# Stores of attention results move from SyncE's DMA queue to GpSimd's, and their readers wait for the landing

## The chip, the cores and the metric

The kernel runs on one core of a Trainium2 chip. Five engines work side by side, each through its own list of instructions, strictly in order: TensorE (PE; its weight loads are listed apart as PEld), VectorE (DVE), ScalarE (ACT), GpSimd (POOL) and SyncE (SP), which computes nothing and issues DMA transfers. The metric is the device time of one execution in microseconds (us). Three runs of the kernel before gave 1774.26, 1767.66 and 1772.58 us, a median of 1772.58.

## What is computed

One decoder layer over 2048 tokens of width 1024: RMSNorm, one projection to 3724 columns, four groups of four attention heads with different rules (A, B, C, D), a SiLU gate, an output projection, and the residual sum.

```python
h = rms_norm(x, norm_w[layer]) @ w_in[layer]
o_a = dilated_attention(...)   # A: windows 128, 512, 2048 with strides 1, 4, 16, merged by their softmax sums
o_b, _ = banded_attention(...) # B: sliding window of 128, shared keys, learned sinks
o_c = diff_attention(...)      # C: two causal softmax maps, p0 - lam * p1, then a norm per head
o_d = nsa_attention(...)       # D: compressed + selected top-16 blocks + window of 512, sigmoid gates
y = concatenate([merge(o_a), merge(o_b), merge(o_c), merge(o_d)]) * silu(silu_gate)
x = x + y @ w_out[layer]
```

## The kernel before

Activations and weights are split into a high and a low part (`xh`, `xl`, `wb`), so that each product is three matmuls. GpSimd makes `xh` and `xl` from the loaded input tile `xt` (lines 571 and 577), two pairs for each tile of 128 tokens. The projection of a group runs over 16 such tiles; its queries, keys, values and gates go to DRAM and are read back by the attention.

The attention runs as units of one to four query tiles: scores on TensorE, bias and row maximum on VectorE (line 952), exp on ScalarE (1050), transposes of the probabilities on TensorE (393), their split into `ph` and `pl` on ScalarE and VectorE (399 and 403), and products with the values (422). In group C VectorE also combines the two maps (line 1066, with two inputs in SBUF). At a unit's end the result is turned (435), and GpSimd scales it (448; in C also 1099 to 1102, in D also 1553, in A 1887 and 1890). Then it is stored to one of four DRAM tensors: `yC`, `yD`, `yA`, `yB`, 32, 32, 8 and 16 stores. The last part, the output projection, loads them back as `xt<-yC`, `xt<-yD` and so on, multiplies them with the gate on GpSimd (2113), turns them and multiplies with `w_out` (2159). Its first half (C and D) writes a partial sum `acc_d`, its second half (A and B) adds to it and writes the output.

The order of everything is set while the program is built. A planner in the kernel keeps a clock for each engine in a dictionary `T`, adds an assumed duration for each instruction that it emits, and always picks the next step whose inputs are ready by these clocks. `defer(ready, f)` queues work for an assumed time. The projection of the next group, and at the end the output projection, are "fillers": they are emitted where attention has nothing ready. So a changed clock anywhere changes the order on all engines; the hardware then follows that order, waiting by semaphores where an assumption was wrong. The stretches of the trace: projection of C to about 120 us, attention C beside the projections of C, D and A to about 720, D's window and compressed branches beside A's and B's to about 1040, D's selected branch beside B's to 1350, A's wide windows beside the output projection to about 1510, A's window of 128 and B to 1720, and the rest of the output projection to the end.

Every DMA is issued by `mv` on SyncE's queue (line 156). SyncE waits there until what the transfer reads has been written and the place that it writes is free, and what stands behind waits with it. To lessen this the planner emits a result's store late: in C and D 4500 ns (`LATE`) after it should be ready by the clocks, in A and B 1500 ns (`LATE2`), or when the next unit closes. `dstored`, `astored` and `stored` count the stores issued; the output projection's loads of `y` are emitted once the counts are complete. They then stand behind the stores in the same queue, and wait there for their landing.

Of the kernel before, what the change touches and what calls it, by code (L numbers as in the profile page):

```python
# [102 lines left out]
def tile_hybrid_heads(ctx, tc, a):  # L103
# [50 lines left out]
    def mv(dst, src, after=0.0):  # L154

        sy.dma_start(dst, src)
        T["SP"] = max(T["SP"], T["PE"], after) + 475.0
        run = 4.0 * min(dst.shape[-1], src.shape[-1])
        T["DMA"] = max(T["DMA"], T["SP"] + 650.0) + 4.0 * math.prod(dst.shape) / run * (4.7 + 0.0456 * run) / 16
        return T["DMA"] + 1900.0  # L160

    filling = [False]
# [326 lines left out]
    def dv(t):  # L489
        return t.rearrange("(t p) c -> p t c", p=128)  # L490
# [493 lines left out]
    def group_c():  # L984
      with tc.tile_pool(name="cs", bufs=1) as cs, tc.tile_pool(name="cw", bufs=2) as cw:
# [34 lines left out]
        def make(h, t0):  # L1020
# [66 lines left out]
            def close(ot):  # L1087
                O = cw.tile([128, 2, 64], F32, name="O")
                rd = cw.tile([128, 4], F32, name="rd")
                V.reciprocal(rd[:, 0:2], den[:, :, 0])  # L1090
                e = o_turn(ot, 2, O, rd[:, 0:2])
                sq = KK[1][:, 0:64]
                ss = rd[:, 2:4]

                def rest():
                    for i in range(2):
                        A.activation(sq, O[:, i], AF.Square, accum_out=ss[:, i:i + 1])
                    e2 = op("ACT", 2 * av(64, 1), e)
                    G.tensor_scalar(ss, ss, 1.0 / 64, EPS, op0=OP.mult, op1=OP.add)
                    G.tensor_tensor(ss, ss, expo[:, :2], op=OP.pow)  # L1100
                    G.tensor_tensor(O, O, ss.unsqueeze(2).broadcast_to([128, 2, 64]), op=OP.mult)
                    G.tensor_tensor(O, O, subln.unsqueeze(1).broadcast_to([128, 2, 64]), op=OP.mult)
                    e3 = op("POOL", 1966.0, e2)
                    last.append(defer(e3 + (LATE if (h, t0) != (3, 14) else 0.0), lambda: mv(dv(y_d["C"])[:, t0:t0 + 2, h * 64:h * 64 + 64], O)))
                while last:
                    last.pop(0).run()
                last.append(defer(e, rest))
# [131 lines left out]
    def group_d():  # L1239
      with tc.tile_pool(name="dk", bufs=1) as dk:  # L1240
# [132 lines left out]
        with tc.tile_pool(name="ds", bufs=1) as ds_:  # L1373
# [133 lines left out]
          with tc.tile_pool(name="dx", bufs=2) as dx:  # L1507
            start("A", before_a(), more)
            PR = Rows([dx.tile([128, S], F32, name="prow%d" % i, bufs=1) for i in range(4)])
            def make(h, t0):  # L1510
# [33 lines left out]
                def close(ot):  # L1544
# [8 lines left out]
                    G.tensor_tensor(O, O, yp, op=OP.add)  # L1553
                    e = op("POOL", 420.0, e)

                    def store():
                        mv(dv(y_d["D"])[:, ts, h * 64:h * 64 + 64], O)
                        dstored[t0] = dstored.get(t0, 0) + 1
                    closing(defer(e + (LATE if (h, t0) != (3, 14) else 0.0), store))

                u = unit(dx, s1, causal_banks(rows, t0, lambda b: VS[:, b, :]), 2,
                         lambda bi: max(rt[0], rt[1]) if len(rt) == 2 else None, close)
# [53 lines left out]
    def group_ab():  # L1616
      with tc.tile_pool(name="aw", bufs=2) as aw, tc.tile_pool(name="as", bufs=1) as as_:
# [241 lines left out]
            u["v"] = lambda vb: As[m][2][:, q0 + vb - As[m][7], :]  # L1859
            return u  # L1860

        pend, pend2 = [], []

        def join(m, q0, h, e):
            R, Y = As[m][3], As[m][8]
# [15 lines left out]
            def two(e1):  # L1881
# [9 lines left out]
                e3 = op("POOL", 2027.0, e2)  # L1891

                def go():
                    e = mv(dv(y_d["A"])[:, q0:q0 + 4, h * 64 - 64:h * 64 + 64], Y)
                    release(As[m - 1][5], e)
                    release(As[m][5], e)
                    astored[q0] = astored.get(q0, 0) + 2
                    defer(T["PE"] + 500.0, a_more)
                if h % 2:
                    pend2.append(defer(e3 + LATE2, go))  # L1900
            while pend2:
                pend2.pop(0).run()
            defer(e, one)


# [23 lines left out]
        def make_b(n):  # L1929
# [48 lines left out]
            def close(ot):  # L1978
# [10 lines left out]
                op("DVE", 300.0, e)  # L1989
                e = o_turn(ot, 4, O, den)  # L1990

                def store():
                    mv(dv(y_d["B"])[:, t0:t0 + 2, g * 128:g * 128 + 128], O.rearrange("p (t j) d -> p t (j d)", j=2))
                    stored[t0] = stored.get(t0, 0) + 1
                while blast:
                    blast.pop(0).run()
                blast.append(defer(e + LATE2, store))

            need = lambda: max(at("s"), bready.get((g, t0), INF))
            u = unit(as_, [(need, lambda: scores(0)), (need, lambda: scores(1))], banks, 4,  # L2000
# [64 lines left out]
    def out_proj():  # L2065
# [76 lines left out]
        for n, (t, halves, _, dst) in enumerate(JOBS):  # L2142
            at_["part"] = p0
            prepare()
            for c in range(2):
# [22 lines left out]

                def go(xr=xr, hk=hk, t=t, c=c, dst=dst):
                    release(hk, mv(dst[t * 128:(t + 1) * 128, c * 512:(c + 1) * 512], xr))  # L2170
                defer(e, go)
            p0 += len(halves)

    with tc.tile_pool(name="first", bufs=1) as fp:
# [63 lines left out]
```

## Time and profile before

| | us |
|---|---|
| median of three runs | 1772.58 |
| the profiled execution | 1773.27 |
| its span, first to last instruction | 1771.5 |
| PE busy | 1709.5 (97%) |
| DVE busy | 1338.3 (76%) |
| ACT busy | 1072.3 (61%) |
| POOL busy | 692.8 (39%) |
| DMA, share of 16 engines | 55.8% |

An engine is busy when at least one of its instructions runs. The matmuls overlap (one begins while the last drains), so a busy TensorE is not one at its peak. A wait is the idle time of an engine just before an instruction, put down to what came last of the things the instruction waited for. SyncE's waits are listed apart, since its queue has no busy time. The chain of waits follows the work that ended last back to the start.

### The profile page before, as it was taken

The page shows a single profiled execution, that of the slowest core. Times are in us where ns is not written, and L with a number is a line of the kernel's source. Part 1 is how long each engine was busy: PE and PEld are TensorE (multiplying, and loading weights), DVE is VectorE, ACT ScalarE, POOL GpSimd, SP SyncE. Part 2 cuts the span into 40 slices and gives each one's busy share as a digit, 9 for nine tenths or more (in the row PEclk, how much of TensorE's full clock was granted, in tenths as well). Part 3 has the DMA queues.
Part 4 walks back from the last instruction along what each step waited for, and adds up shares of the span by engine and source line. Part 5 has one row for each costly group of instructions (what it writes and reads, how often), then busy time and mean ns, then how long its engine had stood idle before and what let it go on. Part 6 is the DMA issues. An engine that isn't in the chain of part 4 may idle for free.

```text
span 1771.5 us, 31769 instructions
## 1 busy us (share of the span) xinstructions
PE 1709.5 (97%) x10035; PEld 1503.3 (85%) x10035; DVE 1338.3 (76%) x4072; ACT 1072.3 (61%) x2588; POOL 692.8 (39%) x841
## 2 busy tenths in 40 slices
PE   7999999999998999899999999999999999999999
PEld 5878878888887889788888889899979999789987
DVE  4446689898999998488747868888366876888873
ACT  4345466656776756467646656777356776576651
POOL 4567554544544554211255552222521112433331
PEclk9999999999999999899999999999999999999999
DMA  7763554444445424642367533232375778999986
GB/s 246 223 198 108 184 171 144 121 118 139 116 143 159 146 91 152 188 117 88 125 194 226 170 108 96 59 97 85 105 238 169 233 226 259 278 313 311 320 283 213
DMA packets 283480, 308.24 MB, mean 174 GB/s; under 512 B 80256, under 2 KB 201216, under 8 KB 282640
## 3 DMA queue, kind: packets, MB, share of 16 engines
q1 hardware_dynamic: 283312, 306.21, 55.8%
q8 instruction: 80, 1.31, 0.3%
q14 instruction: 88, 0.72, 0.1%
HBM read 219.47 MB, written 86.92 MB: 173 GB/s over the span
## 4 chain that ended last, share of the span: by engine, by line
PE 51%; DVE 3%; issue 1%; DMA 1%; ACT 1%; POOL 0%; SPq 0%; DVEq 0%; POOLq 0%
PE j L840 11%; PE j L2159 9%; PE o L422 9%; PE pt L393 8%; PE s L1646 4%; PE s L950 4%; PE pt L435 3%; PE s L1336 1%; PE pt L2123 1%; PE s L1948 1%; PE s L1435 1%; PE pt L741 0%; DVE pl L403 0%; PE j L1164 0%; DMA xt<-in_xt_dram 0%
## 5 line engine op out<-in xcount | busy, mean ns | idle before, releaser
L840 PE MATMUL j<-wb,xh 128*128 128x512 f32 (+2 forms) x2048 | 618.2, 382 | 18.8 <-DVE wb L622 9.6
L840 PEld LDWEIGHTS j<-wb,xh 128*128 128x128 f32 x2048 | 373.1, 190 | 67.4 <-DVE wb L622 14.5
L840 PE MATMUL j<-wb,xl 128*128 128x512 f32 (+2 forms) x1024 | 385.4, 376 | 0.6 <-POOL xl L577 0.6
L399 ACT ACTIVATE ph<-pt 128x512 fp32r<-128x512 f32 (+4 forms) x486 | 266.0, 575 | 123.5 <-PE pt L393 117.0
L403 DVE TENSOR_TENSOR pl<-pt,ph 128x512 fp32r<-128x512 f32 (+4 forms) x486 | 311.9, 658 | 38.1 <-ACT ph L399 37.2
L840 PEld LDWEIGHTS j<-wb,xl 128*128 128x128 f32 x1024 | 194.3, 190 | 25.7 <-POOL xl L577 1.2
L679 POOL TENSOR_TENSOR ss<-ss,expo 128x6 f32<-128x6 f32 (+2 forms) x64 | 117.4, 1835 | 169.2 <-DVE ss L677 155.3
L577 POOL TENSOR_TENSOR xl<-xt,xh 128x512 fp32r<-128x512 f32 x112 | 149.2, 1333 | 9.3
L371 ACT ACTIVATE ot<-o 128x512 f32<-128x512 f32 (+1 forms) x160 | 81.5, 509 | 106.4 <-PE o L422 105.9
L571 POOL TENSOR_SCALAR xh<-xt 128x512 fp32r<-128x512 f32 x128 | 84.6, 661 | 134.2 <-DMA xt<-in_xt_dram 65.5
L950 PE MATMUL s<-keys,Q 128*128 128x512 f32 (+3 forms) x320 | 113.6, 400 | 12.7 <-DVE mx L952 6.1
L2113 POOL TENSOR_TENSOR xt<-xt,sq 128x512 f32<-128x512 f32 x32 | 41.3, 1290 | 184.2 <-PE s L1646 66.2
L952 DVE CUSTOM_DVE_ANT_0 prow<-s,Hs 128x512 f32<-128x512 f32 (+3 forms) x160 | 95.1, 604 | 19.3 <-PE s L950 18.8
L1066 DVE SCALAR_TENSOR_TENSOR pa<-pb,ra,pa 128x1024 f32<-128x1024 f32 (+4 forms) x96 | 107.5, 1147 | 2.3
L660 ACT ACTIVATE stqk<-j 128x512 f32<-128x512 f32 x64 | 38.2, 597 | 113.5 <-PE j L840 111.0
L952 DVE CUSTOM_DVE_ANT_0 pa<-s,H 128x512 f32<-128x512 f32 (+3 forms) x160 | 93.8, 603 | 14.0 <-PE s L950 11.3
L952 DVE CUSTOM_DVE_ANT_0 pb<-s,H 128x512 f32<-128x512 f32 (+3 forms) x160 | 93.1, 603 | 7.2 <-PE s L950 6.5
L1662 ACT ACTIVATE ap<-ap,AO 128x128 f32<-128x128 f32 (+1 forms) x192 | 86.4, 456 | 17.7 <-DVE AO L1656 17.5
L1050 ACT ACTIVATE pa<-pa,nm 128x128 f32<-128x128 f32 (+7 forms) x64 | 76.9, 1202 | 31.5 <-DVE nm L958 31.0
L674 DVE TENSOR_REDUCE ss<-sq 128x6 f32<-128x384 f32 (+2 forms) x64 | 39.3, 614 | 69.9 <-ACT sq L664 69.9
L435 PE MATMUL pt<-ident,ot 128*128 128x128 f32 x512 | 85.0, 278 | 3.1 <-ACT ot L371 2.6
L1050 ACT ACTIVATE pb<-pb,nm 128x128 f32<-128x128 f32 (+7 forms) x64 | 76.8, 1200 | 16.5 <-DVE nm L958 16.3
(267 smaller groups left out, 4207.4 us busy)
## 6 DMA issues: line engine op xcount, KB each, us to landing
xt<-in_xt_dram SPq DMA_DIRECT2D x128, 256.0 KB, 3.3
xr<-in_x_dram SPq DMA_DIRECT2D x16, 512.0 KB, 5.4
Q<-tqC SPq DMA_DIRECT2D x64, 128.0 KB, 3.4
DQ<-tqD SPq DMA_DIRECT2D x16, 512.0 KB, 4.8
raw<-gate_d SPq DMA_DIRECT2D x32, 256.0 KB, 4.2
stqk<-in_x_dram SPq DMA_DIRECT2D x32, 256.0 KB, 4.8
acc_d<-stqk SPq DMA_DIRECT2D x32, 256.0 KB, 4.5
stqk<-acc_d SPq DMA_DIRECT2D x32, 256.0 KB, 4.5
```

The source lines that it names most:

```text
L393: PE.transpose(ps[:rows, x * 128:(x + 1) * 128], src(), ident)
L399: A.activation(ph[:rows, :n], ps[:rows, :n], AF.Copy)
L403: V.tensor_tensor(pl[:rows, :n], ps[:rows, :n], ph[:rows, :n], op=OP.subtract)
L422: PE.matmul(u["po"][:, c0:c0 + wd], lhsT=lhsT(), rhs=x[:rows, col:col + wd], start=u["k"] == 1, stop=u["k"] == total, skip_group_check=True)
L435: PE.transpose(ps[:, i * 128:(i + 1) * 128], ot[:, i * 128:(i + 1) * 128], ident)
L577: G.tensor_tensor(l, xt, h, op=OP.subtract)
L679: G.tensor_tensor(ss[:, :nh], ss[:, :nh], expo[:, :nh], op=OP.pow)
L840: PE.matmul(ps[:, :n], lhsT=xx[:, ks], rhs=W[k][ww][:, lo:hi], start=(k == 0 and i == 0), stop=(k == KT - 1 and i == 2))
L950: PE.matmul(ps[:, :n], lhsT=q(), rhs=k[:, k0:k0 + n], start=(i == 0), stop=(i == np_ - 1))
L952: V.tensor_tensor_reduce(st["row"][:, k0:k0 + n], ps[:, :n], rev(H, t * 128 + 127 - k0, n), 1.0, LOW, OP.add, OP.max, st["mx"][:, ci:ci + 1])
L1050: A.activation(row[:, :nk], row[:, :nk], AF.Exp, bias=nm, accum_out=den[:, i, m:m + 1])
L2159: PE.matmul(ps, lhsT=xx[:, ks], rhs=OW[half, (k, c)][ww], start=(x == 0 and k == 0 and i == 0), stop=(x == len(halves) - 1 and k == 3 and ...
```

## The change

Three edits. (1) A new helper `mg` issues a DMA on GpSimd's queue and charges the planner's clock of GpSimd 1000 ns for it. The 88 stores of `yC`, `yD`, `yA` and `yB` use it, right behind the GpSimd instruction that makes the result, with no `LATE`, no `LATE2` and no wait for the next unit. (2) The counts rise, and `landed` runs, at the time at which the transfer should have landed by the planner's clocks (`mg`'s return value), not when it is issued. (3) The output projection's stores of `acc_d` and of the output, still on SyncE, are emitted 1500 ns later, but for the last two jobs of 32.

```diff
+    def mg(dst, src):
+
+        G.dma_start(dst, src)
+        T["POOL"] += 1000.0
+        run = 4.0 * min(dst.shape[-1], src.shape[-1])
+        T["DMA"] = max(T["DMA"], T["POOL"] + 650.0) + 4.0 * math.prod(dst.shape) / run * (4.7 + 0.0456 * run) / 16
+        return T["DMA"] + 1900.0
...
-                    last.append(defer(e3 + (LATE if (h, t0) != (3, 14) else 0.0), lambda: mv(dv(y_d["C"])[:, t0:t0 + 2, h * 64:h * 64 + 64], O)))
+                    mg(dv(y_d["C"])[:, t0:t0 + 2, h * 64:h * 64 + 64], O)
...
-                    def store():
-                        mv(dv(y_d["D"])[:, ts, h * 64:h * 64 + 64], O)
+                    e = mg(dv(y_d["D"])[:, ts, h * 64:h * 64 + 64], O)
+
+                    def landed():
                         dstored[t0] = dstored.get(t0, 0) + 1
-                    closing(defer(e + (LATE if (h, t0) != (3, 14) else 0.0), store))
+                    defer(e, landed)
...
                 def go():
-                    e = mv(dv(y_d["A"])[:, q0:q0 + 4, h * 64 - 64:h * 64 + 64], Y)
+                    e = mg(dv(y_d["A"])[:, q0:q0 + 4, h * 64 - 64:h * 64 + 64], Y)
                     release(As[m - 1][5], e)
                     release(As[m][5], e)
-                    astored[q0] = astored.get(q0, 0) + 2
+
+                    def landed():
+                        astored[q0] = astored.get(q0, 0) + 2
+                    defer(e, landed)
                     defer(T["PE"] + 500.0, a_more)
                 if h % 2:
-                    pend2.append(defer(e3 + LATE2, go))
-            while pend2:
-                pend2.pop(0).run()
+                    go()
...
-                defer(e, go)
+                defer(e + (LATE2 if n < len(JOBS) - 2 else 0.0), go)
```

B's store changes as D's does. All engines' orders change with the clocks; the matmuls are the same ones.

GpSimd's queue in group C's attention beside D's projection, before: `xh` and `xl` belong to the projection, `O` and `rd` to a unit of C, `stqk` and `ss` to the norm of D's queries.

```order
L448 TENSOR_TENSOR O<-O,rd 128x128
L1099 TENSOR_SCALAR rd<-rd 128x2
L1100 TENSOR_TENSOR rd<-rd,expo 128x2
L1101 TENSOR_TENSOR O<-O,rd 128x128
L1102 TENSOR_TENSOR O<-O,subln 128x128
L571 TENSOR_SCALAR xh<-xt 128x512
L577 TENSOR_TENSOR xl<-xt,xh 128x512
```

The same queue at such a place now (line numbers are larger by 8 to 9 in the changed file).

```order
L456 TENSOR_TENSOR O<-O,rd 128x128
L579 TENSOR_SCALAR xh<-xt 128x512
L585 TENSOR_TENSOR xl<-xt,xh 128x512
L1107 TENSOR_SCALAR rd<-rd 128x2
L1108 TENSOR_TENSOR rd<-rd,expo 128x2
L1109 TENSOR_TENSOR O<-O,rd 128x128
L1110 TENSOR_TENSOR O<-O,subln 128x128
L164 DMA yC<-O 128x2x64
L687 TENSOR_TENSOR ss<-ss,expo 128x6
```

The store of `yC` now stands between GpSimd's own instructions, in front of the next one that the projection needs.

SyncE's queue in D's selected branch, before: `Qs` and `Qb` are the queries of a coming unit, `Hs` its bias rows, `yps` the other branches' sum that GpSimd adds at a unit's end, `yD` the result.

```order
L156 DMA Qs<-tqD 128x512
L156 DMA Qb<-tqD 64x512
L156 DMA yD<-Os 128x2x64
L156 DMA yps<-yp_d 128x2x64
L156 DMA yD<-Os 128x2x64
L156 DMA yps<-yp_d 128x2x64
L156 DMA yD<-Os 128x2x64
L156 DMA Hs<-fvec 128x512
L156 DMA Hs<-fvec 128x1536
```

The same queue in the same branch now.

```order
L156 DMA Qs<-tqD 128x512
L156 DMA Qb<-tqD 64x512
L156 DMA yps<-yp_d 128x2x64 x2
L156 DMA xt<-in_xt_dram 128x512
L156 DMA yps<-yp_d 128x2x64
L156 DMA gate_d<-gst 128x416
L156 DMA Qs<-tqD 128x512
L156 DMA Qb<-tqD 64x512
```

The loads of this branch no longer have a store of a result among them.

## Rows read from the trace of the kernel before

**Rows 1.** The profile's page: span, busy time of each engine, and the engines' shares of the chain that ended last.

```profile
span 1771.5 us, 31769 instructions
PE 1709.5 (97%) x10035; PEld 1503.3 (85%) x10035; DVE 1338.3 (76%) x4072; ACT 1072.3 (61%) x2588; POOL 692.8 (39%) x841
...
PE 51%; DVE 3%; issue 1%; DMA 1%; ACT 1%; POOL 0%; SPq 0%; DVEq 0%; POOLq 0%
```

**Rows 2.** Busy time by stretch of the trace: from:to, length, then busy us and count for PE, PEld, DVE, ACT and POOL, the granted clock of PE as a share of full speed, the DMA engines' share and GB/s.

```profile
200.00:400.00 200.00, 190.29 (x1067) 165.00 (x1066) 180.35 (x464) 126.21 (x260) 98.29 (x113) 0.99 0.46 138
400.00:600.00 200.00, 190.15 (x1090) 165.90 (x1090) 185.75 (x511) 135.17 (x295) 94.81 (x120) 0.98 0.47 140
...
1000.00:1200.00 200.00, 200.00 (x1329) 181.51 (x1328) 158.01 (x509) 132.34 (x274) 69.06 (x102) 1.00 0.31 94
...
1500.00:1600.00 100.00, 95.33 (x618) 84.20 (x618) 86.85 (x274) 64.97 (x193) 33.29 (x41) 0.98 0.92 286
1600.00:1700.00 100.00, 100.00 (x678) 90.41 (x677) 85.71 (x314) 70.79 (x216) 34.67 (x49) 1.00 1.02 315
```

**Rows 3.** The waits of SyncE's queue over the whole run: who waited for what, us in total, times, the longest.

```profile
SPq L156 <- POOL xl L577: 115.1, 39, 10.8
SPq L156 <- POOL Os L1553: 112.5, 26, 9.3
SPq L156 <- PE s L950: 88.2, 24, 13.0
SPq L156 <- DVE stqk L2165: 61.6, 29, 5.6
...
SPq L156 <- POOL O L1102: 42.3, 12, 9.9
...
SPq L156 <- POOL O L448: 19.4, 3, 12.2
...
SPq L156 <- POOL Os L448: 6.7, 1, 6.7
```

**Rows 4.** The transfers of single tensors on SyncE's queue: ns to issue one, shortest, median and longest, and when the first and the last began.

```profile
L156 SPq DMA_DIRECT2D yC<-O x32: 366/378/671, 142.4 to 713.6; - x32
...
L156 SPq DMA_DIRECT2D yD<-Os x32: 359/363/539, 1042.2 to 1350.1; - x32
...
L156 SPq DMA_DIRECT2D yA<-AO x8: 370/371/394, 1536.9 to 1719.4; - x8
...
L156 SPq DMA_DIRECT2D yB<-gst x16: 370/374/459, 1527.9 to 1719.9; - x16
...
L156 SPq DMA_DIRECT2D xt<-in_xt_dram x128: 327/382/2462, 0.7 to 1281.4; - x128
```

**Rows 5.** The waits of TensorE over the whole run, those put down to a DMA or to GpSimd: us in total, times, the longest.

```profile
PE j L1164 <- DMA xt<-in_xt_dram: 2.4, 1, 2.4
...
PE s L950 <- DMA Q<-tqC: 1.6, 2, 1.2
PE pt L741 <- POOL stqk L683: 1.4, 2, 0.9
PE s L950 <- DMA VS<-vvC: 1.4, 1, 1.4
PE s L1336 <- DMA DQ<-tqD: 1.2, 1, 1.2
...
PE s L950 <- DMA H<-fvec: 1.0, 1, 1.0
...
PE pt L2123 <- DMA BQ<-tqB: 0.8, 1, 0.8
...
PE o L422 <- DMA VW<-vvD: 0.6, 1, 0.6
PE j L840 <- POOL xl L577: 0.6, 1, 0.6
```

**Rows 6.** The chain of waits from 1510 to 1600 us: start, length, what.

```profile
1520.53 0.34 SPq L156
1520.86 0.05 issue
1520.91 3.56 DMA wb<-tqA
...
1587.67 0.52 SPq L156
...
1588.24 1.44 SPq L156
...
1590.80 3.76 DMA BQ<-tqB
```

**Rows 7.** GpSimd's costliest groups, shapes kept apart: line, operation, tiles, shapes, count, busy us in all, mean ns of one, idle us before them.

```profile
L1100 POOL TENSOR_TENSOR rd<-rd,expo 128x2 f32<-128x2 f32 x32 | 26.6, 833 | 2.7
```

**Rows 8.** VectorE's line 1066 in order of time: one alone at 160.80 us, two back to back at 225.99 us; then GpSimd at that second place.

```profile
160.80 1.28 DVE L1066 SCALAR_TENSOR_TENSOR pa<-pb,ra,pa 128x1024 f32<-128x1024 f32 x1
...
225.99 3.75 DVE L1066 SCALAR_TENSOR_TENSOR pa<-pb,ra,pa 128x1024 f32<-128x1024 f32 x2
...
226.04 1.30 POOL L577 TENSOR_TENSOR xl<-xt,xh 128x512 fp32r<-128x512 f32 x1
227.30 2.03 POOL L683 TENSOR_TENSOR stqk<-stqk,ss 128x512 f32<-128x512 f32 x1
```

**Rows 9.** GpSimd and then TensorE in order of time around 472 us, where the split of an input tile comes closest to its use in D's projection.

```profile
470.31 0.46 POOL L1102 TENSOR_TENSOR O<-O,subln 128x128 f32<-128x128 f32 x1
470.74 0.62 POOL L571 TENSOR_SCALAR xh<-xt 128x512 fp32r<-128x512 f32 x1
471.44 2.02 POOL L577 TENSOR_TENSOR xl<-xt,xh 128x512 fp32r<-128x512 f32 x1
...
474.47 0.70 PE L840 MATMUL j<-wb,xh 128*128 128x512 f32 x2
475.01 0.39 PE L840 MATMUL j<-wb,xl 128*128 128x512 f32 x1
```

More of the change, by code (lines that the diff above doesn't have):

```diff
@@ L1860, in make_a1 @@
             return u
-        pend, pend2 = [], []
+        pend = []
         def join(m, q0, h, e):
@@ L1990, in close, with landed @@
                 e = o_turn(ot, 4, O, den)
-                def store():
-                    mv(dv(y_d["B"])[:, t0:t0 + 2, g * 128:g * 128 + 128], O.rearrange("p (t j) d -> p t (j d)", j=2))
+                e = mg(dv(y_d["B"])[:, t0:t0 + 2, g * 128:g * 128 + 128], O.rearrange("p (t j) d -> p t (j d)", j=2))
+                def landed():
                     stored[t0] = stored.get(t0, 0) + 1
-                while blast:
-                    blast.pop(0).run()
-                blast.append(defer(e + LATE2, store))
+                defer(e, landed)
             need = lambda: max(at("s"), bready.get((g, t0), INF))
```

## The prediction, made before the changed kernel was timed

> **What bounds the kernel now.** I read the page's first part and the chain of waits first. TensorE is busy for 1709.5 of 1771.5 us, and 51% of the chain is TensorE's own work; no other engine or queue holds more than 3% of it [rows 1]. The most that any change of waiting can give is therefore the 62 us in which TensorE is idle, plus what hides in overlapping matmuls. I read next where these 62 us lie, from the windows: 9.7 and 9.85 us in 200 to 400 and 400 to 600, where VectorE is busy for 180 and 186 of 200 us; nothing in 1000 to 1200, the stretch that holds most of D's stores; 4.7 us in 1500 to 1600, where the DMA engines' share is 0.92 [rows 2]. Last I read the waits of SyncE's queue, on which all stores stand, and TensorE's waits that are put down to a DMA or to GpSimd. The first are long, the second short, and that contrast decides the forecast.
>
> **What it removes.** SyncE issues 88 transfers less: 32 of `yC` at 0.378 us, 32 of `yD` at 0.363, 8 of `yA` at 0.371 and 16 of `yB` at 0.374, which is 12.1 + 11.6 + 3.0 + 6.0 = 32.7 us [rows 4]. The queue's waits for the results go too: 112.5 + 6.7 for D's, 42.3 + 19.4 for C's, 180.9 us in all [rows 3]. That is a tenth of the span, but only of a queue. What of it lies on TensorE's path is what TensorE waits for late loads: in C's attention 1.6 for `Q`, 1.4 for `VS` and 1.0 for `H`, 4.0 us [rows 5]; in D's selected branch none, since the longest single waits of SyncE (9.3 us) stand in a stretch where TensorE is busy for 200.00 of 200 us [rows 2, 3]; in A's and B's last stage the chain leaves TensorE twice for SyncE and a load, at 1520.53 for 0.34 + 0.05 + 3.56 us and at 1587.67 for SyncE's issues and a `BQ` load of 3.76 us [rows 6], against 4.7 us of idle time in that hundred [rows 2]. So the two places where an earlier load could count hold 4.0 + 4.7 = 8.7 us.
>
> How much of it comes back? The results' stores are not the queue's only stops. 115.1 us of waiting for `xl` (a free input buffer) and 88.2 us for scores (a free query buffer) stay [rows 3], and a load freed from behind a store runs into the next of them. In the last stage the DMA engines themselves are at 0.92 to 1.02 [rows 2], so a transfer issued earlier may land no earlier. The bounds are 0 and 8.7 us; without a row that shows a load alone behind a store I take the middle, 4.4 us. In D's branch I count nothing: SyncE was waiting there under a TensorE that never stopped.
>
> The other waits of SyncE that go are those for the output projection's sum, 61.6 us in 29 times [rows 3]: with 1500 ns more the queue meets a finished sum. The loads behind them are the same as above in the last stage, and the jobs after 1600 us run with TensorE busy for 100.00 of 100 us [rows 2], so this adds nothing of its own. If the cover were gone, it would be at the very end, where the last two jobs keep their old time, so I count nothing there either. A sum's buffer is held 1.5 us longer; there are five of them and a job takes two, so the load for the next job still finds one free.
>
> **What it adds.** 88 issues on GpSimd. No row of before shows one. The nearest rows are SyncE's issue of the same stores, 0.36 us, the longest issue of a load on SyncE, 2.46 us [rows 4], and on GpSimd an instruction of 256 results, as many as `yC` has separate runs, 0.83 us [rows 7]. I take 0.83, with the ends 0.36 and 2.46: 88 of them are 73 us (32 to 216), which lifts GpSimd from 692.8 to 766 us, 43% of the span. GpSimd is not the bound at either end (909 us at the upper). What counts is what stands behind a store on GpSimd: in C and D the input pair `xh` and `xl`, the norms of the queries, and the next unit's result. TensorE now waits for GpSimd for 1.4 us on `stqk` and 0.6 on `xl` [rows 5], so nearly all of it is ready early. The closest that I found in D's projection is the pair whose `xl` ends at 471.44 + 2.02 = 473.46 us and is used at 475.01: 1.55 us of cover; its `xh` ends at 471.36 and is used at 474.47 [rows 9]. A store in front of it at 0.83 us leaves 0.7 us; at 2.46 us TensorE waits 0.9 us. One such pair in the 32 tiles beside C's stores makes this 0 at my value and under 1 us at the upper end, and I count 0.4 us for the places where the cover is thinner than in D. The output store's own wait on GpSimd for the instruction before it is inside the same bounds.
>
> **The counts that rise at the landing.** The output projection's loads of `y` are emitted some microseconds later. They are fillers with two parts prepared ahead, and the stretch that uses the last of them (1600 to 1700) has no idle TensorE [rows 2]. This costs nothing, and SyncE no longer stands still before such a load until the store in front has landed.
>
> **The sum.** -4.4 + 0.4 = -4.0 us. The profiled execution took 1773.27 us, 1.8 us above its span and 0.7 above the median of the three runs, so it stands for them. 1773.27 - 4.0 = 1769.3; I predict 1769. The new order of all engines by itself I count as zero with 6 us to either side: an estimate, two thirds of the 9.0 us for which TensorE now waits for DMA in all (added up under rival B), about what other orders can lose or win at such places. The forecast's own range is 1763 to 1775.
>
> **Rivals.** A: the freed queue moves nothing. For it speak the 203.3 us of waiting that stay in SyncE's queue [rows 3] and a TensorE that is busy 97%; against it the two places in the chain that end in SyncE and a load [rows 6]. Then only the issue time of 32.7 us is saved, on a queue that bounds nothing: 1773 us. The Trainium skill has a rule for this (DMA: Bandwidth & Descriptors, section "Issuing engines are not separate DMA queues"): the same 16 engines move the data whoever issues it, and a second issuer saves only the time that issuing takes on the sequencer. By that rule this rival would be the forecast; the rows show 180.9 us of standing still beside 32.7 us of issuing, which the rule leaves out.
>
> B: the freed queue moves more than the waits named after a DMA. Late loads also make ScalarE, VectorE and GpSimd late. For it speaks that all of TensorE's waits for DMA together are 2.4 + 1.6 + 1.4 + 1.2 + 1.0 + 0.8 + 0.6 = 9.0 us [rows 5]; with the 4.7 us of the last stage, less the 0.8 that stand in both, 12.9 us would go: 1760 us. Against it: the 2.4 for `xt`, 1.2 for `DQ` and 0.6 for `VW` lie at the change from C to D, behind no store of a result but the last of C.
>
> C, on the other side: a store issued by GpSimd holds up VectorE. Line 1066 takes 1.28 us alone, but two in a row beside GpSimd's split take 3.75 us, so the first is held up by about 1.15 us (3.75 less twice 1.28); GpSimd's next instruction then runs for 2.03 us [rows 8]. Two instructions of these engines that read SBUF thus keep each other waiting. If an issue on GpSimd does the same, the stores of C between 200 and 600 us (32 in 571 us [rows 4], so some 22 in 400) cost VectorE 22 x 1.15 = 25 us where it is idle for only 33.9 of 400 us [rows 2]. Some of that idle time is bound to other waits, so I let half of the 25 us reach TensorE: +12.5, 1786 us. It decides from a hold of about 1 us at each store; below 0.4 us (9 us in all) it disappears in VectorE's idle time. Against it: a transfer's data do not pass through GpSimd's own instruction. The Trainium skill warns of the opposite direction (SBUF — State Buffer, section "SBUF: two separate sides"): descriptors of a DMA issued from GpSimd are written by GpSimd itself, and a VectorE instruction that holds the port they share keeps them from being written, so that the store starts late. No run here shows such a store; by that rule the stores land later, which the waits on the landing would hide.
>
> **How the numbers follow.** The forecast gets 0.42, A 0.22, B 0.22, C 0.14. A measurement of this kernel tells about 0.5% from no change, 8.9 us of 1772.58: faster is below 1763.7, slower above 1781.4. The forecast with its 6 us gives 0.05 faster, 0.36 same, 0.01 slower; A 0.01, 0.20, 0.01; B 0.19, 0.03, 0; C 0, 0.02, 0.12. Together 0.25, 0.61 and 0.14. The range goes down past B by 5 us and up past C by 2: 1755 to 1788.
>
> **What would show it.** Right: SyncE's waits for `Os` and `O` gone, those for `xl` and for scores no shorter or longer; GpSimd busy for more than 692.8 us or with longer idle stretches, and TensorE's waits for GpSimd still under 4 us; TensorE busy for over 95.33 us in 1500 to 1600, and 200 of 200 in D's branch. Rival C would show as VectorE's line 1066 (its number in the changed file is larger) with a mean above that of before, and as TensorE waiting for it. The prediction is wrong if TensorE's idle time moves by more than 9 us either way, above all in a stretch where no store of a result stands.

## The result, and the profile after

The changed kernel takes 1788.1 us (median of 4 runs, 1787.2 to 1789.7) against 1770.1 for the kernel before on the same chip: the ratio is 1.0100, with a 95% interval from 1.0075 to 1.0125, so it is 18 us slower. 1769 was predicted, with a range from 1755 to 1788. Line numbers below are those of each run's own file: the changed kernel stands 8 to 9 lines lower than before, line 1066 is 1074.

The page of after, its first two lines and its two main DMA queues (packets, MB, share of 16 engines):

```profile
span 1786.3 us, 31849 instructions
PE 1711.7 (96%) x10035; PEld 1501.8 (84%) x10035; DVE 1338.1 (75%) x4072; ACT 1072.9 (60%) x2585; POOL 756.5 (42%) x929
...
q1 hardware_dynamic: 257328, 297.82, 53.4%
q0 software_dynamic: 3456, 8.39, 1.5%
```

TensorE's work is what it was (1709.5 in [rows 1]); its idle time grew from 62.0 to 74.6 us. GpSimd has 63.7 us more, and its lines of stores say why (busy us, mean ns of one, idle us before them and its cause):

```profile
L164 POOL DMA_DIRECT2D yC<-O x32 | 25.3, 791 | 9.5 <-POOL O L1110 9.5
L164 POOL DMA_DIRECT2D yD<-Os x32 | 24.3, 759 | 10.8 <-POOL Os L1561 8.0 <-issue 1.6 <-DVE dens L1558 0.6
L164 POOL DMA_DIRECT2D yB<-gst x16 | 12.0, 748 | 4.7 <-POOL gst L456 4.4 <-DMA BV<-vvB 0.3
L164 POOL DMA_DIRECT2D yA<-AO x8 | 6.3, 791 | 2.4 <-POOL AO L1899 1.5 <-DMA xt<-yA 0.6 <-DMA wb<-tqA 0.3
```

One store holds GpSimd for 0.75 to 0.79 us, twice SyncE's issue [rows 4], and before it GpSimd waits 0.3 us (9.5 / 32) for its own last instruction to finish. The waits of SyncE's queue that answer to [rows 3]:

```profile
SPq L156 <- PE s L958: 164.5, 27, 14.5
SPq L156 <- POOL xl L585: 155.7, 39, 13.3
SPq L156 <- DVE stqk L2174: 79.8, 35, 10.5
```

The waits for `Os` and `O` are gone from the head of the list, and the others grew: scores from 88.2 to 164.5, `xl` from 115.1 to 155.7, even the output sum that edit 3 was to spare, from 61.6 to 79.8. TensorE's own waits, as in [rows 5]:

```profile
PE s L958 <- DVE mx L960: 16.6, 18, 1.7
...
PE s L958 <- DMA Q<-tqC: 4.6, 4, 1.3
...
PE s L1443 <- issue: 2.2, 1, 2.2
...
PE pt L749 <- POOL stqk L691: 1.1, 2, 0.9
...
PE j L848 <- POOL xl L585: 0.6, 1, 0.6
```

Those for GpSimd did not grow; those for VectorE's row maximum `mx` did, from 8.9 to 16.6 us. So the place to look is the order of the work: where does TensorE lose? I use one measure for that below, called **excess**: for each matmul, the time from its start to the next one's start, less the larger of 109 ns and 0.445 ns per column + 4.5 ns, which is how closely they follow one another where nothing is awaited; summed by branch. Half clock shows in it as well as waiting. All of it is from one execution of each kernel. The columns: the kernel before; early stores by SyncE and by GpSimd in the old order (h2, h1); C's part alone (f1), and with one load earlier (k1); after; after's order with SyncE's stores (e2).

| branch (us in before) | before | h2 | h1 | f1 | k1 | after | e2 |
|---|---|---|---|---|---|---|---|
| C's attention (118 to 690) | 47.9 | 43.9 | 55.3 | 43.3 | 41.6 | 43.8 | 41.7 |
| turn to D (690 to 735) | 9.4 | 9.1 | 7.9 | 11.7 | 11.0 | 12.1 | 10.4 |
| D's window and behind it (735 to 923) | 16.6 | 14.9 | 15.8 | 18.4 | 18.8 | 19.3 | 19.6 |
| compressed (923 to 1034) | 8.0 | 8.3 | 8.2 | 14.1 | 9.4 | 14.2 | 10.5 |
| selected (1034 to 1347) | 11.4 | 14.5 | 13.2 | 15.2 | 15.0 | 14.3 | 13.7 |
| A, wide (1347 to 1507) | 33.8 | 34.9 | 33.7 | 33.7 | 38.7 | 34.0 | 33.6 |
| A, B and the end (from 1507) | 8.0 | 9.4 | 12.2 | 8.4 | 8.4 | 14.3 | 27.1 |

A caution on the first row: three other runs that have the sequence of before in C and its late stores by SyncE (edit 3 alone, D's part alone, A's and B's alone) show 43.9, 43.8 and 42.9 there, and h2 43.9, so the 47.9 of the profile before is high by chance, and the 4 us that after seems to gain in C are none. What after loses lies behind C: 2.7 at the turn, 2.7 to the compressed branch, 6.2 in it, 2.9 in the selected one, 6.3 at the end, though no store of a result stands in the stretch from 735 to 1034.

### The profile page after: what moved, and what is told of

It reads as the page before. It is cut to its first block, busy times and chain, and to the rows that moved or that the text cites. A ratio compares the mean times of both kernels' runs of the same rounds, so it can differ in the third digit from the quotient of the medians.

```text
span 1786.3 us, 31849 instructions
## 1 busy us (share of the span) xinstructions
PE 1711.7 (96%) x10035; PEld 1501.8 (84%) x10035; DVE 1338.1 (75%) x4072; ACT 1072.9 (60%) x2585; POOL 756.5 (42%) x929
## 3 DMA queue, kind: packets, MB, share of 16 engines
q1 hardware_dynamic: 257328, 297.82, 53.4%
q0 software_dynamic: 3456, 8.39, 1.5%
## 5 line engine op out<-in xcount | busy, mean ns | idle before, releaser
L687 POOL TENSOR_TENSOR ss<-ss,expo 128x6 f32<-128x6 f32 (+2 forms) x64 | 118.1, 1845 | 179.3 <-DVE ss L685 152.5
L2122 POOL TENSOR_TENSOR xt<-xt,sq 128x512 f32<-128x512 f32 x32 | 41.2, 1286 | 180.9 <-DVE sq L2119 77.1
L1074 DVE SCALAR_TENSOR_TENSOR pa<-pb,ra,pa 128x1024 f32<-128x1024 f32 (+4 forms) x96 | 104.7, 1118 | 2.3
L1538 ACT ACTIVATE prow<-prow,nm 128x128 f32<-128x128 f32 (+7 forms) x64 | 76.8, 1201 | 18.5 <-DVE nm L966 18.2
```

The source lines that it names most:

```text
L687: G.tensor_tensor(ss[:, :nh], ss[:, :nh], expo[:, :nh], op=OP.pow)
L1074: V.scalar_tensor_tensor(rows[i][:, k0:k0 + n], part[i][:, k0:k0 + n], ra[:, 1:2], rows[i][:, k0:k0 + n], op0=OP.mult, op1=OP.add)
```

## Experiments 1: the issuing engine and the order, taken apart

Each time is a median, each ratio is against runs of the kernel before on the same chip. The first run keeps the old order of TensorE, VectorE and ScalarE to the row and lets GpSimd issue at the old, late places:

```diff
-    lambda: mv(dv(y_d["C"])[...], O)     # and so for D, A and B
+    lambda: mg(dv(y_d["C"])[...], O)     # mg: G.dma_start, SyncE's clock charged as before
```

> All four kinds of result stores are issued by GpSimd, but at the places and in the instruction order of the kernel before: TensorE, VectorE and ScalarE have the identical sequence. The order theory (the new order of the instructions costs the 18 us, the issuing engine itself next to nothing) expects 1764 to 1773 us: the 1770.1 of before, less at most the 4.4 us of late loads that the prediction took. The issue theory (GpSimd's issue and its 64 us more of work hold up the chain, or its descriptor writing disturbs VectorE) expects 1780 to 1788 us, with VectorE's line 1066 (1074 here) above 1147 ns in the mean or TensorE's waits for GpSimd well above 4 us.

1774.1 us, 1.0025 (1.0014 to 1.0036): no gain, a loss of 4 us. SyncE's queue of this run:

```profile
SPq L156 <- PE s L958: 155.9, 24, 13.8
SPq L156 <- POOL xl L585: 139.2, 40, 10.8
SPq L156 <- DVE stqk L2173: 92.1, 38, 9.6
SPq L156 <- DVE vst L717: 75.4, 15, 16.3
```

The sequence of the computing engines is the same, the waits for `Os` are gone, and the time stands before the next things in the queue instead: this queue is ahead of the work and waits somewhere in any case. The second run is the reverse, after's order and early places with SyncE as the issuer:

```diff
 def mg(dst, src):
-    G.dma_start(dst, src)
+    sy.dma_start(dst, src)
```

> The changed kernel's identical sequence on TensorE, VectorE and ScalarE, and its early places of the stores, but the stores issued by SyncE again, which then waits for the unfinished result with the loads queued behind it. The order theory expects 1788 us or more: all that the new order costs, plus what the waits of SyncE's queue cost (the chain rows of before show single waits of up to a few us, so 1788 to 1815). The issue theory expects it to fall back towards the kernel before, 1770 to 1780 us.

1796.6 us, 1.0156 (1.0136 to 1.0177). In this order GpSimd's stores are worth 8.5 us against SyncE's, and the loss stays without them. By the table SyncE's stores are better in C and the compressed branch and lose 13 us at the end, where TensorE's two longest waits, both for VectorE's `pl`, are 3.9 and 3.8 us. The second can be followed back to SyncE's queue:

```profile
1634.38 0.36 SPq L164 DMA_DIRECT2D yA<-AO  x1
...
1642.89 0.69 DVE L2174 TENSOR_TENSOR stqk<-j,stqk 128x512 f32<-128x512 f32 x1 [4.84 <-DMA stqk<-acc_d]
```

Two stores, of `yB` at 1632.28 and of `yA`, had held the queue for 1.1 and 1.7 us until their results were ready. The load of the partial sum stands behind them, is issued at 1637.54 and lands at 1642.79. VectorE waits for it, and TensorE waits 3.75 us for VectorE. So in this order SyncE's waits for results (162.1 us for C's, 145.8 for D's, 36.0 for B's) do cost time. The third edit alone on the kernel before:

```diff
-                defer(e, go)
+                defer(e + (LATE2 if n < len(JOBS) - 2 else 0.0), go)
```

> The kernel before with the third edit alone: output stores are deferred by LATE2, the last two excepted. If that edit costs (output stores land late, buffers come free late, the tail is longer) 1778 to 1788 us; if it is worth nothing, as the prediction had it, 1767 to 1774; if it removes the 61.6 us of SyncE's waits for the output tile to a gain, 1760 to 1767.

1769.4 us, 0.9999 (0.9984 to 1.0013): nothing. And another order with nothing of the change in it, `LATE = 4400.0` for 4500.0:

> The kernel before with nothing of the change, only the planner's constant LATE at 4400 in place of 4500, which gives TensorE another sequence over large parts of the program. If a different order of the same work is by itself worth as much as the change's loss, this lies away from 1770 by 5 to 20 us, to either side; if orders of this planner are all alike, within 4 us of 1770.1, and then the loss of the change must come from something specific in it.

1776.9 us, 1.0047 (1.0028 to 1.0066): 100 ns in one constant of the planner are worth 6 us by the medians and 8 by the ratio.

## Experiments 2: the parts

Each part of the change alone on the kernel before, as its hunk of the diff has it, with `mg` and its charge of 1000 ns:

> The change's first part alone: C's 32 result stores by GpSimd at once after the result, with the planner's POOL charge of 1000 ns; D, A, B and the output stores as in the kernel before. It rewrites the order of nearly the whole program (some 3,400 of TensorE's rows differ). If the loss sits in the order that C's part brings, 1780 to 1790 us; if C's part brings only its own gain in C's branch (the 4.1 us of excess that went there between the kernels), 1764 to 1772; if the loss needs the parts together, near 1770.

> D's 32 stores alone in the new manner, with their count at landing; some 690 of TensorE's rows differ, all after the middle of the program. Order theory: as large as the order is changed, so 1768 to 1778 us. If counts at landing are what costs (work that needs a stored block is let go too late), 1778 to 1788 us.

> A's 8 and B's 16 stores alone in the new manner, with their counts at landing; only the last stretch from about 1350 us on is rewritten. If the last stretch's own changes cost (between before and after it showed 4.6 us more excess from 1507 us on and 1.8 us more behind the last attention matmul), 1775 to 1780 us; if they gain, as the prediction's 4.7 us of late loads had it, 1765 to 1769; without an effect 1768 to 1773.

C's part: 1781.1 us, 1.0068 (1.0041 to 1.0095). D's: 1779.1, 1.0062 (1.0041 to 1.0083). A's and B's: 1772.8, 1.0019 (1.0004 to 1.0033). They add up to 1.0149, more than the 1.0100 of the whole, so they are no shares of one sum. Next the whole change with the planner's charge for a store on GpSimd at 780 ns, which is what it really takes, and then at 900:

```diff
-        T["POOL"] += 1000.0
+        T["POOL"] += 780.0     # second run: 900.0
```

> The whole change, but the planner charges GpSimd 780 ns for a store, which is what the trace of after measures, in place of 1000; nothing else is edited, and some 4,100 of TensorE's rows move. If the loss is a matter of which order the planner happens to fall into, this lies 4 us or more away from 1788, to either side; if it comes from a part of the change as such (early stores, counts at landing, late output stores), it stays at 1784 to 1791 us. If the wrong charge itself misleads the planner, it is faster, 1770 to 1780.

> The whole change with the planner's charge for a GpSimd store at 900 ns, between the 1000 of the change and the 780 of the earlier run. If the time followed the charge in an orderly way, it would lie between 1788 and 1809, near 1797. If each order is a draw of its own, it may lie anywhere from 1770 to 1810, and nothing binds it to lie between the two.

1808.6 us (1.0223, 1.0195 to 1.0250) and 1810.6 us (1.0238, 1.0218 to 1.0257). A truer charge makes it 20 us slower, and 900 does not lie between 780 and 1000. Two parts undone inside the change, edit 3 and the counts at landing (`dstored`, `astored`, `stored` raised at the issue again):

```diff
-                defer(e + (LATE2 if n < len(JOBS) - 2 else 0.0), go)     # first run
+                defer(e, go)
-                    defer(e, landed)                                     # second run, and so for A and B
+                    dstored[t0] = dstored.get(t0, 0) + 1
```

> The changed kernel without its third edit (output stores at once, as before). In the kernel before that edit alone was worth 0 (0.9999). If it costs in the new order, where the output projection stands later and the last 46 us show 1.8 us more excess, this is 1780 to 1785 us; if it is worth nothing there too, 1786 to 1790; if it gains in the new order, 1790 to 1796.

> The changed kernel with the counts of stored blocks of D, A and B taken at the issue of the store, as before, and not at its landing. If work let go too late is a part of the loss, 1776 to 1784 us; if the counts are worth nothing by themselves, as the prediction had it, it stays within some 5 us of 1788, by the new order that this edit brings (some 680 of TensorE's rows move).

1803.3 us (1.0193, 1.0177 to 1.0208) and 1792.6 us (1.0132, 1.0115 to 1.0148). Edit 3 is worth nothing in the old order and seems to be worth 15 us in the new one: the likely reading is that the order which comes with it is measured there, and not the edit. The excess without it is that of after up to the end of the selected branch and 17 us more from there on. Undoing the counts gains nothing.

## Experiments 3: what the new order loses at one place

Busy time by 10 us at the head of the compressed branch (as in [rows 2]; PE's busy us are the first figure behind the length, its granted clock the third from the end), before:

```profile
920.00:930.00 10.00, 9.22 (x56) 8.10 (x57) 7.71 (x28) 7.33 (x24) 4.90 (x7) 1.00 1.01 340
930.00:940.00 10.00, 8.86 (x53) 6.73 (x52) 7.58 (x32) 7.65 (x19) 3.67 (x4) 1.00 0.99 324
940.00:950.00 10.00, 10.00 (x62) 8.77 (x61) 7.84 (x35) 6.17 (x27) 3.26 (x4) 1.00 0.99 291
950.00:960.00 10.00, 10.00 (x56) 7.95 (x55) 7.50 (x25) 5.99 (x22) 6.35 (x8) 1.00 0.44 137
```

and after:

```profile
920.00:930.00 10.00, 5.69 (x36) 4.45 (x34) 6.06 (x27) 4.50 (x15) 4.29 (x5) 0.96 0.99 322
930.00:940.00 10.00, 10.00 (x41) 8.53 (x42) 3.60 (x8) 4.96 (x15) 1.91 (x2) 0.70 0.94 293
940.00:950.00 10.00, 10.00 (x65) 9.15 (x64) 7.43 (x39) 6.43 (x28) 4.77 (x6) 1.00 0.69 204
950.00:960.00 10.00, 9.53 (x43) 7.15 (x42) 6.77 (x39) 6.70 (x25) 3.46 (x4) 0.66 0.44 130
```

TensorE stands still for 4.3 of 10 us, and in the next 30 us the clock is at 1.2 GHz in two stretches (0.70 and 0.66 in the mean, where 1.00 is 2.4 GHz). A busy time of 10.00 hides this: the count falls from 53 to 41 and from 56 to 43. Up to 0.4 + 3.0 + 3.4 = 6.8 us of full-clock time are lost, against 6.2 us more excess. The wait of 2.2 us before `s L1443` ends at 926.28; the list of waits names no releaser, but `s` reads `DQ`, and the load of `DQ`, issued at 919.90, lands after 6.3 us, at 926.19. In before it is issued 2.0 us earlier, lands after 4.8 us at 922.66, and `s` starts at 922.86 without a wait. SyncE's queue in after, and then in before:

```profile
918.38 0.42 SPq L156 DMA_DIRECT2D tqA<-th  x1
918.86 0.42 SPq L156 DMA_DIRECT2D tqA<-tl  x1
919.32 0.48 SPq L156 DMA_DIRECT2D HC<-fvec  x1
919.90 0.43 SPq L156 DMA_DIRECT2D DQ<-tqD  x1
```

```profile
917.34 0.42 SPq L156 DMA_DIRECT2D HC<-fvec  x1
917.86 0.38 SPq L156 DMA_DIRECT2D DQ<-tqD  x1
```

The new order has put loads and two stores of the projection ahead of it. So I changed that place alone, in SyncE's queue, with the planner's clocks and all other engines untouched:

```diff
+    nmv[0] += 1                       # counts SyncE's transfers
+    if 620 <= nmv[0] - 1 <= 623:      # raw, raw, tqA<-th, tqA<-tl
+        heldq.append((dst, src))
+    else:
+        sy.dma_start(dst, src)
+    if nmv[0] - 1 == 625:             # DQ is out: now the four
+        while heldq: sy.dma_start(*heldq.pop(0))
```

> The changed kernel with only SyncE's queue touched, at one place near 916 us: the load of DQ, for which TensorE waits 2.2 us at the head of the compressed branch, and the last HC are issued ahead of two raw loads and two tqA stores that stand before them; all other engines keep their sequence. If a late load there, and the half clock granted after it, are a part of the loss (the branch's 14.2 us of excess against 8.0 before), the wait goes, the 930 to 960 us stretch runs nearer to full clock, the branch falls to 8 to 11 us of excess and the time to 1782 to 1786 us. If the wait only moves to the next late thing (the raw loads, which VectorE splits for the projection), the excess stays at 13 to 15 us and the time at 1787 to 1789.

1784.9 us, 1.0087 (1.0072 to 1.0102), 3.3 us off, and the branch's excess is 11.0:

```profile
920.00:930.00 10.00, 7.34 (x41) 6.16 (x41) 5.75 (x27) 6.17 (x22) 4.09 (x4) 0.86 0.95 318
930.00:940.00 10.00, 10.00 (x62) 8.58 (x60) 6.14 (x28) 5.54 (x18) 3.20 (x4) 0.97 0.91 294
940.00:950.00 10.00, 9.53 (x60) 8.55 (x58) 7.88 (x45) 6.65 (x25) 3.42 (x4) 1.00 0.85 254
950.00:960.00 10.00, 9.58 (x56) 7.70 (x56) 7.77 (x39) 6.35 (x24) 6.37 (x9) 1.00 0.39 114
```

The wait for `DQ` is gone, the longest wait for VectorE's `wb` (the weights made from the raw loads) has grown from 1.4 to 2.0 us, and the second half-clock stretch is gone. Both answers that I had expected are in it. The same cure on C's part alone, whose order is the same here:

> C's part alone, as in the run at 1781.1 us, with the load of DQ at the head of the compressed branch moved ahead of two raw loads and two tqA stores in SyncE's queue; no other engine's sequence changes. If the late DQ and the half clock behind it are a real part of the loss, the same 2 to 4 us come off as in the changed kernel (1788.1 to 1784.9): 1777 to 1779 us, with the branch's excess down from 14.1 to about 11. If that gain was chance, 1780 to 1783.

1776.9 us, 1.0045 (1.0029 to 1.0060) against 1.0068: 4 us, in medians, and the branch is at 9.4. Each pair of intervals overlaps, but both runs go the same way and the branch shows it both times: by the medians one place in a queue is worth about as much as the whole gain that was forecast.

## Experiments 4: is it the charge, the place, or the engine?

C's part alone again, in three versions: with the charge to SyncE's clock, late with the charge to GpSimd's, and with no charge to either.

```diff
-        T["POOL"] += 1000.0                                # first run
+        T["SP"] = max(T["SP"], T["PE"]) + 475.0
-        mg(dv(y_d["C"])[...], O)                           # second run
+        last.append(defer(e3 + LATE, lambda: mg(dv(y_d["C"])[...], O)))
-        T["POOL"] += 1000.0                                # third run
```

> C's stores alone, early and by GpSimd as in the run of C's part alone (1781.1), but the planner charges them to SyncE's clock as before the change. If it is the charge of 1000 ns to GpSimd's clock that leads the planner to the worse order, this falls back to 1766 to 1774 us; if it is the early place in the order, it stays at 1778 to 1785; if any order other than the one before is a draw with a loss in the mean, it is 1775 to 1800 without a relation to either.

> C's stores alone by GpSimd with the planner's charge of 1000 ns to GpSimd's clock, but LATE behind the result as before the change. If the charge leads to the worse order, 1778 to 1785 us; if the early place does, 1766 to 1774; if orders are draws, 1775 to 1800 without a relation to either.

> C's stores alone, early and by GpSimd, and the planner charges no issuing engine at all. If the charge to GpSimd is at fault, 1766 to 1774 us, as with the charge to SyncE; if the early place is, 1778 to 1785; if orders are draws, 1775 to 1800 without a relation to the other two.

1792.3 us (1.0128, 1.0104 to 1.0152), 1789.3 (1.0125, 1.0098 to 1.0151) and 1787.8 (1.0103, 1.0083 to 1.0124): two of them worse than C's part as it stands, the third no better. Neither charge nor place alone is the cause; every new order that C's part brings is slower, and all three have half clock after 920 us and 12.8 to 20.5 us of excess in the compressed branch. Of the 13 other sequences of TensorE timed here, all but that of edit 3 alone (some 800 of its 10,035 rows stand elsewhere) are slower than the one before. Why that one is so good is not shown.

Last, the change's act on the machine without its order: the stores right behind the results, in the old order, by GpSimd and then by SyncE.

```diff
+    G.dma_start(dv(y_d["C"])[...], O)     # at the result; second run: sy.dma_start
-    last.append(defer(e3 + LATE, lambda: mv(dv(y_d["C"])[...], O)))
+    last.append(defer(e3 + LATE, lambda: paid(dv(y_d["C"])[...], O)))   # the planner's charge alone
```

> All result stores issued by GpSimd right behind the instruction that makes the result, as in the change, but in the instruction order of the kernel before: TensorE, VectorE and ScalarE keep their sequence to the row, the planner charges SyncE as before, counts and edit 3 as before. This is the change's act on the machine without its order. Theory of the order: 1765 to 1774 us, close to the 1774.1 with late GpSimd stores or some us better, since nothing waits for a store. If early issue by GpSimd itself is what costs (its 0.75 us issues in front of splits and chains that TensorE waits for), 1780 us or more.

> The kernel with early stores in the old order, but SyncE issues them: TensorE, VectorE, ScalarE and GpSimd have the sequence of the kernel before to the row, and only SyncE's queue meets each store earlier, so that it stands waiting for the unfinished result with loads behind it. If the 9 us that early GpSimd stores cost over late ones are GpSimd's own (0.79 us of issue and a 0.3 us wait in front of its next split), this one is free of them; it then shows what SyncE's waits cost instead: 1772 to 1778 if these are covered, 1785 to 1800 if the loads behind them come late (in the new order SyncE's early stores cost 8.5 us more than GpSimd's).

By GpSimd 1783.4 us, 1.0083 (1.0062 to 1.0104); by SyncE 1771.3 us, 1.0015 (0.9999 to 1.0030). So my theory that only the order costs falls: in one and the same order and place the engine is worth 0.68%, 12 us. SyncE's run also shows that in this order its waits for results cost next to nothing. It waits for them nearly twice as long as the kernel before (180.9 us by [rows 3]); only SyncE's stores in the new order waited longer:

```profile
SPq L1111 <- POOL O L1109: 152.5, 24, 12.7
SPq L1564 <- POOL Os L1561: 137.5, 28, 9.9
```

Where GpSimd's 12 us come from, the table says: C, 55.3 against 43.9, and 2.8 more at the end. GpSimd in order of time at the worst place, first its own stores, then SyncE's:

```profile
607.30 0.46 POOL L1109 TENSOR_TENSOR O<-O,subln 128x128 f32<-128x128 f32 x1
608.06 0.78 POOL L1111 DMA_DIRECT2D yC<-O  x1 [0.29 <-POOL O L1109]
608.86 1.67 POOL L686 TENSOR_TENSOR ss<-ss,expo 128x8 f32<-128x8 f32 x1
...
612.48 2.02 POOL L690 TENSOR_TENSOR stqk<-stqk,ss 128x512 f32<-128x512 f32 x1
```

```profile
599.45 0.46 POOL L1109 TENSOR_TENSOR O<-O,subln 128x128 f32<-128x128 f32 x1
599.86 1.64 POOL L686 TENSOR_TENSOR ss<-ss,expo 128x8 f32<-128x8 f32 x1
...
603.44 1.05 POOL L690 TENSOR_TENSOR stqk<-stqk,ss 128x512 f32<-128x512 f32 x1
```

From the result to `ss` it is 1.56 us with the store (608.86 - 607.30) and 0.41 without. Everything behind it comes 1.1 us later, `stqk` last, which here takes 1 us longer as well. TensorE waits, in the run with GpSimd's stores,

```profile
PE s L957 <- DVE mx L959: 13.1, 18, 2.0
...
PE pt L748 <- POOL stqk L690: 3.8, 4, 2.1
PE pt L2138 <- POOL xt L2128: 3.2, 6, 1.1
PE j L847 <- POOL xl L584: 2.8, 4, 1.0
```

where SyncE's run has 8.5, 1.1, 0.6 and 0.6: together 12.1 us less (10.8 over all of TensorE's waits). The longest wait for VectorE, 2.0 us, also goes back to a store:

```profile
598.60 0.42 DVE L446 TENSOR_REDUCE O<-pt 128x128 f32<-128x256 f32 x1 [2.45 <-DMA yC<-O]
...
599.69 0.50 PE L957 MATMUL s<-keys,Q 128*128 128x512 f32 x1 [2.01 <-DVE mx L959]
```

VectorE wants to write the buffer `O` again and waits until the store that reads it has landed. GpSimd's store of it, issued at 594.67, landed after 3.8 us. SyncE's at the same place landed after 1.6 us, and VectorE did not wait. And at the very pair of [rows 9] two stores stand in front, not one:

```profile
465.60 0.78 POOL L1111 DMA_DIRECT2D yC<-O  x1 [0.29 <-POOL O L1109]
...
470.93 0.79 POOL L1111 DMA_DIRECT2D yC<-O  x1 [0.29 <-DMA xt<-in_xt_dram]
...
472.47 1.28 POOL L584 TENSOR_TENSOR xl<-xt,xh 128x512 fp32r<-128x512 f32 x1
...
473.80 0.50 PE L847 MATMUL j<-wb,xl 128*128 128x512 f32 x1 [0.63 <-POOL xl L584]
```

## Why the prediction was wrong

- **What bounds the kernel**: right. TensorE's work is unchanged and its idle time decides.
- **The late loads, -4.4 us**: wrong for this change. With the waits for results gone (late GpSimd stores in the old order) the time rose by 4 us; with 346 us of them, early and in the old order (152.5 + 137.5 and three smaller groups of 16.5 to 21.1) it rose by 2 to 3, 0 to 5 by the interval. That the freed queue runs into `xl` and the scores was written down, as the ground of rival A; the middle of 0 and 8.7 should have been the 0. The chain's two excursions to SyncE and a load [rows 6] do not stand behind a result that is waited for: the first load is late behind a store of the partial sum, which waits 2.2 us for `stqk`, and the second follows loads. That such waits can cost is seen only in the new order, where GpSimd's stores take 8.5 us less than SyncE's; the prediction had no order in which to look for it. A smaller slip: 4.2 of the 19.4 us on `O L448` [rows 3] stand before an input load and not before a store, so 176.7 us and not 180.9 were C's and D's.
- **The issue on GpSimd, 0.83 us each**: right, 0.75 to 0.79, and GpSimd came to 756.5 us where 766 was said. **Its price, +0.4 us**: wrong, and this is the first step that failed. It is 12 us in the old order. The sum put one store of 0.83 us in front of the pair with 1.55 us of cover [rows 9] and counted no wait there. With its wait of 0.3 us a store costs the line behind it 1.1 us, two of them stand in front of that pair, and TensorE waits 0.63 us for its `xl`; over the run it waits 8 times for `stqk` and `xl`, 6.6 us, where SyncE's run has 3 times and 1.7. That a store also keeps its buffer from VectorE until it has landed was not in the sum at all. TensorE's waits for `stqk` and `xl` [rows 5] were small because GpSimd was on time, which does not say by how much.
- **The new order, 0 with 6 us to either side**: wrong in its size, and the second step that failed; it is the one that shows in the changed kernel, whose 20.8 us of added excess lie behind C, while TensorE's waits for GpSimd are 2.1 us (2.3 before). The change's own order pays back C (55.3 to 43.8 of excess) and loses behind it. Why it pays C back is not shown: with the planner's charge at 900 ns, C has 56.3 again. From the same stores in the old order (1.0083) to after (1.0100) the total moves little, but orders next to it lie at 1793 to 1811, and a change of 100 ns in `LATE` moves 6 to 8 us. An estimate from TensorE's waits for DMA could not show this, for it has no half clock and no late load that an order might bring.
- **Counts at landing and edit 3, 0 each**: edit 3 alone is 0.9999; undoing the counts gains nothing (1792.6 against 1788.1). Inside the new order neither can be told from what another order brings by itself.
- **Rivals.** A was right about SyncE's queue and wrong about the end. The Trainium skill's rule that it cited (DMA: Bandwidth & Descriptors, section "Issuing engines are not separate DMA queues") agrees with these traces: the DMA engines' share is 53.4 + 1.5% against 55.8% before, and no run with GpSimd's stores is faster than before. The 12 us are a cost on the new issuer, of what stands behind the store there. B fell. C forecast the time, 1786, by the wrong way: line 1074 has a mean of 1118 ns in after, against 1147 before. In the old order with early GpSimd stores TensorE's longest wait is for VectorE (13.1 us against 8.5), so VectorE is late there too. It is not held by the stores as C had it: matched one by one with SyncE's run, the 261 VectorE instructions that run beside a store by GpSimd take 1.1 us less in all. The longest of these waits goes back to a store's landing (above); the others were not followed.
- **The signs to look for**: TensorE's waits for GpSimd stayed under 4 us, and `Os` and `O` left SyncE's queue, both as written, and the kernel still lost 18 us. TensorE's idle time moved by 12.6 us, over the 9 that were named. 200 of 200 in D's branch became 198.23, and 95.33 in 1500 to 1600 became 96.15. The sentence that held is the last: the prediction is wrong if idle time moves in a stretch where no store stands.

What stays open: how the 18 us divide. The early place by itself, with SyncE in the old order, is 0.15%. If the engine is changed next, it is 0.68% for the engine and 0.17% for the order (with the counts and edit 3), the latter within the intervals of nothing; if the order is changed next, it is 1.41% for the order and -0.56% for the engine. Both ways are measured, so the two do not add. Of the order's part only the place at the head of the compressed branch was traced to a cause, 3 to 4 us by medians whose intervals overlap; what makes the rest is open. No version timed here beats the kernel before; early stores by SyncE in the old order come up to it.

## What to carry to other kernels

Before a wait of a queue is counted as a loss, look at what stands next in that queue: 346 us of waiting for results on SyncE cost at most 0.3% in one order here, and in another, with 344 us for C's, D's and B's, a load that stood behind two such waits came late and held TensorE for 3.75 us. Before work is moved to an engine with idle time, add what it holds up there, its wait for the instruction before included, ask how long its buffer stays taken, and look at what is next on that engine in each unit, not at its busy share. Where a planner sets the order from estimated costs, time the act in the old order as well as in the new one, and a neighbouring order or two, before the edit is given the credit or the blame.

## What the runs showed of the hardware

A store issued by GpSimd lands later than the same store by SyncE at the same place in the same order: 2.2 against 1.6 us from issue to landing for `yC`, 2.1 against 1.6 for `yD` (medians of 32, early stores in the old order). And it moves the 8.39 MB in far fewer pieces: 3,456 packets on GpSimd's queue, while SyncE's lost 25,984 (283,312 before); the time did not gain by it.
